# Decoder layer on one core: seven products in four of eight pairs of three input-projection sections, with five low parts made by an adding transfer

## The chip, the cores and the metric

One core of a Trainium2 chip runs the whole program. The metric is the time of one execution in microseconds of device time. The kernel before takes 1112.39 us (median of three runs, 1111.93 to 1112.93).

## The reference

One layer: block-sparse attention (with 256 positions it is one causal block), then a SwiGLU network, each followed by a LayerNorm. What matters here is the first product, `x @ w_qkv` in float32.

```
q, k, v = jnp.split(x @ w_qkv, 3, axis=-1)          # x 256 x 2048, w_qkv 2048 x 6144
o = moba_attention(q * HEAD_DIM ** -0.5, k, v, rel_bias.T)
x = layer_norm(ALPHA * x + o @ w_o, ln1_g, ln1_b)
x = layer_norm(ALPHA * x + (silu(x @ w_gate) * (x @ w_up)) @ w_down, ln2_g, ln2_b)
```

## The kernel before, in words

**Products.** Every float32 operand is split into a high part `hi` (rounded to float32r by ScalarE) and a low part `lo` = value minus `hi` (VectorE). A product is three matmuls of 128x512 into one PSUM bank: hi by hi, lo by hi, hi by lo (lines 317 to 319, or 381 to 385 where plain sections write them out).

**Sections and pairs.** The input projection has six sections Q0 to Q5; each makes two 512-wide column chunks for 256 rows of x. The inner dimension is walked in eight *pairs* p0 to p7 of two 128-deep steps. Sections Q1, Q2 and Q3 (the table `SEVEN`) and the gate sections f1 to f10 of the feed-forward part work on combined operands: an ordinary pair there takes eight products (four in each of two *blocks*), a pair listed in the section's table `st` takes seven (three in its first block, four in its second). Results land in seven accumulators, numbered 1 to 7; at the end of a section `sums_1` (accumulators 1, 6, 7), `sums_2` (2, 4) and `sums_3` (5, 3) add them up on VectorE. Accumulators 1, 6 and 7 are written by the seven-product pairs alone, so `sums_1` is queued behind the last such pair.

**Weights.** An ordinary pair is prepared by `plain`: SyncE loads two raw tiles of 512 KB, `split_piece` splits each: ScalarE writes `wh_...`, VectorE subtracts and writes `wl_...`. A seven-product pair is prepared in three steps, `quad_sums` (four additions of 128x512, lines 280 to 283, into `t13` and `t24`), `quad_raw` (splits into `gq`, `uq`) and `quad_low` (splits into `aq`, `bq`). In gate sections f1 to f10 the second chunk of pairs 0 and 5 (`ADDED`) has its low part made in another way: ScalarE writes `hi`, then minus `hi` into the low tile, and a transfer issued by GpSimd adds the weights from memory onto it.

**Left operands.** `combine_x(p)` makes differences of x for each pair, three small VectorE additions and one split more for a pair in the table (lines 331 to 333). It runs during Q0.

**Order.** All is issued from one list of blocks; each engine executes its instructions in that order and waits on semaphores. A step of preparation is queued a fixed number of blocks ahead of the pair's first block: in Q sections 3 for an ordinary pair, 4, 3 and 2 for the three steps of a seven-product pair; in the gate sections after f1 it is 5, and 6, 5 and 4. Tiles of 128x1024 come from 38 buffers, raw tiles from 6.

Of the kernel before, what the change touches and what calls it, by code (L numbers as in the profile page):

```python
# [40 lines left out]
SQK, SV = {0: 0, 1: 2, 2: 4, 3: 5}, {1: (0, 1), 3: (2, 3)}  # L41
SEVEN = (1, 2, 3)
KEEP = 2
ST_Q = (1, 3, 5)
ST_F = (1, 3, 4, 6)
ADDED = (0, 5)
WARM = 9
LEAD = {("d", 0): 6, ("d", 1): 4}
# [4 lines left out]
def decoder_layer(ctx: ExitStack, tc: tile.TileContext, x, xt, rel_bias, w_qkv, w_o, g1, b1, gb1,  # L53
# [9 lines left out]
    def p4(shape, dt, name):  # L63
        return sb.tile(shape, dt, tag="p4", bufs=P4, name=name)
# [19 lines left out]
    def f32(t):  # L84
        return t.bitcast(F)

    def split(hi, lo, src):
        nc.scalar.activation(hi, src, AF.Copy)  # L88
        nc.vector.tensor_tensor(lo, src, f32(hi), op=OP.subtract)  # L89
# [85 lines left out]
        hi, lo = hS[kt // 4]  # L175
        return hi[:, kt % 4, m * P:(m + 1) * P], lo[:, kt % 4, m * P:(m + 1) * P]

    xC, x1C = {"st": ST_Q}, {"st": ST_F}
    Q = [Sec(f"q{n}", [(w_qkv, 4 * i + g) for i, g in pair], 8, x_lhs, xC if n in SEVEN else None)
         for n, pair in enumerate(QKV)]  # L180
    WO = [Sec(f"o{i}", [(w_o, 2 * i + c) for c in range(2)], 8, o_lhs) for i in range(2)]
# [69 lines left out]
    def load_piece(s, p, c):  # L251
        w, col = s.chunks[c]
        r = sb.tile([P, 2, CW], F, tag="raw", bufs=RAW, name=f"r_{s.name}_{p}_{c}")
        src = w[p, col]
        if s is not Q[0] or p:
            nc.sync.dma_start(r, src)
        s.raws[p, c] = r, src

    def split_piece(s, p, c):
        if (p, c) not in s.raws:  # L260
            load_piece(s, p, c)
        r, src = s.raws.pop((p, c))
        hi = p4([P, 2, CW], R, f"wh_{s.name}_{p}_{c}")
        lo = p4([P, 2, CW], R, f"wl_{s.name}_{p}_{c}")
        if s.st == ST_F and c == 1 and p in ADDED:
            nc.scalar.activation(hi, r, AF.Copy)
            nc.scalar.activation(lo, f32(hi), AF.Copy, scale=-1.0)
            nc.gpsimd.dma_start(lo, src, accum_op=OP.add)
        else:
            split(hi, lo, r)  # L270
        s.pieces[p, c] = (hi, lo)
# [33 lines left out]
    def plain(s, p):  # L305
        if s is Q[0]:
            load_x(p, slice(0, 2))
            split_x(p, slice(0, 2))
        for c in range(len(s.chunks)):
            split_piece(s, p, c)  # L310
# [402 lines left out]
    for g in range(4):  # L713
        s = Q[SQK[g]]
# [74 lines left out]
    s = Q[0]  # L789
# [14 lines left out]
    for t, blk in enumerate(blocks):  # L804
        for f, a in pre.get(t, []):
            f(*a)
        while n < len(order) and order[n][0] <= t:
            _, _, p, what, ss = order[n]
# [54 lines left out]
```

## Time and profile before

| what | value |
|---|---|
| median of three runs | 1112.39 us |
| the profiled execution's own time | 1111.51 us |
| its span in the trace | 1109.7 us |
| TensorE busy | 1090.3 us, 98% |
| VectorE busy | 864.6 us, 78% |
| ScalarE busy | 605.5 us, 55% |
| mean granted TensorE clock | 0.996 of full |

How to read it: the profiled execution ran 0.88 us under the median, and 1.8 us of its time lie outside the span. TensorE is busy nearly all the time, so time is saved where it has fewer matmuls and lost where it stands still.

### The profile page before, as it was taken

The page shows a single profiled execution, that of the slowest core. Times are in us where ns is not written, and L with a number is a line of the kernel's source. Part 1 is how long each engine was busy: PE and PEld are TensorE (multiplying, and loading weights), DVE is VectorE, ACT ScalarE, POOL GpSimd, SP SyncE. Part 2 cuts the span into 40 slices and gives each one's busy share as a digit, 9 for nine tenths or more (in the row PEclk, how much of TensorE's full clock was granted, in tenths as well). Part 3 has the DMA queues.
Part 4 walks back from the last instruction along what each step waited for, and adds up shares of the span by engine and source line. Part 5 has one row for each costly group of instructions (what it writes and reads, how often), then busy time and mean ns, then how long its engine had stood idle before and what let it go on. Part 6 is the DMA issues. An engine that isn't in the chain of part 4 may idle for free.

```text
span 1109.7 us, 13827 instructions
## 1 busy us (share of the span) xinstructions
PE 1090.3 (98%) x4992; PEld 901.2 (81%) x4992; DVE 864.6 (78%) x1154; ACT 605.5 (55%) x781; POOL 27.9 (3%) x36
## 2 busy tenths in 40 slices
PE   9999999999999998999999999999999999999995
PEld 6888888888888886888888888888888888888884
DVE  6899785667778669999899999999899555674446
ACT  6564552555655457757657657657657343353410
POOL 0000000000000000000000000000000000000001
PEclk9999999999999999999999999999999999999998
DMA  9665575465656637868768768768768674578512
GB/s 345 197 235 200 204 242 176 138 196 181 216 190 226 246 107 232 257 228 270 240 195 286 240 208 273 237 207 276 230 233 314 215 316 171 231 281 292 201 38 76
DMA packets 69205, 245.42 MB, mean 221 GB/s; under 512 B 7888, under 2 KB 8336, under 8 KB 69136
## 3 DMA queue, kind: packets, MB, share of 16 engines
q1 hardware_dynamic: 63488, 224.06, 57.1%
q0 software_dynamic: 3488, 12.61, 5.7%
q10 hardware_dynamic: 2160, 7.87, 1.7%
q8 instruction: 39, 0.64, 0.2%
q14 instruction: 30, 0.25, 0.1%
HBM read 234.51 MB, written 9.99 MB: 220 GB/s over the span
## 4 chain that ended last, share of the span: by engine, by line
PE 91%; DVE 3%; ACT 2%; DMA 2%; issue 1%; SPq 0%; POOL 0%; ACTq 0%; POOLq 0%; DVEq 0%
PE acc_f L318 12%; PE acc_f L319 12%; PE acc_f L317 12%; PE acc_d L382 7%; PE acc_d L381 7%; PE acc_d L385 7%; PE acc_q L319 4%; PE acc_q L318 4%; PE acc_q L317 4%; PE acc_q L381 4%; PE acc_q L382 4%; PE acc_q L385 4%; PE acc_o L381 2%; PE acc_o L385 2%; PE acc_o L382 2%; DMA wl_f<-in_w_up 1%
## 5 line engine op out<-in xcount | busy, mean ns | idle before, releaser
L89 DVE TENSOR_TENSOR wl_d<-r_d,wh_d 128x1024 fp32r<-128x1024 f32 x88 | 104.6, 1222 | 71.9 <-ACT wh_d L88 49.5
L381 PE MATMUL acc_d<-wh_d,hh 128*128 128x512 f32 x352 | 137.0, 389 | 0.0
L382 PE MATMUL acc_d<-wl_d,hh 128*128 128x512 f32 x352 | 136.9, 389 | 0.0
L88 ACT ACTIVATE wh_d<-r_d 128x1024 fp32r<-128x1024 f32 x88 | 90.2, 1056 | 74.3 <-DMA r_d<-in_w_down 46.1
L385 PE MATMUL acc_d<-wh_d,hl 128*128 128x512 f32 x352 | 99.9, 389 | 0.0
L89 DVE TENSOR_TENSOR wl_q<-r_q,wh_q 128x1024 fp32r<-128x1024 f32 x76 | 89.6, 1220 | 11.9 <-ACT wh_q L88 11.1
L318 PE MATMUL acc_f<-wl_f,x1h 128*128 128x512 f32 x240 | 93.5, 390 | 3.3 <-DMA wl_f<-in_w_up 3.3
L317 PE MATMUL acc_f<-wh_f,x1h 128*128 128x512 f32 x240 | 95.3, 397 | 0.0
L89 DVE TENSOR_TENSOR wl_f<-r_f,wh_f 128x1024 fp32r<-128x1024 f32 x76 | 89.7, 1218 | 6.4 <-ACT wh_f L88 5.9
L319 PE MATMUL acc_f<-wh_f,x1l 128*128 128x512 f32 x240 | 93.6, 390 | 0.0
L88 ACT ACTIVATE wh_f<-r_f 128x1024 fp32r<-128x1024 f32 x76 | 76.6, 1050 | 6.3 <-ACT hT L675 3.2
L385 PEld LDWEIGHTS acc_d<-wh_d,hl 128*128 128x128 f32 x352 | 66.1, 188 | 13.7
L381 PEld LDWEIGHTS acc_d<-wh_d,hh 128*128 128x128 f32 x352 | 66.1, 188 | 13.7
L88 ACT ACTIVATE wh_q<-r_q 128x1024 fp32r<-128x1024 f32 x76 | 75.9, 1048 | 2.3 <-DMA r_q<-in_w_qkv 2.1
L382 PEld LDWEIGHTS acc_d<-wl_d,hh 128*128 128x128 f32 x352 | 66.1, 188 | 13.7
L381 PE MATMUL acc_q<-wh_q,xh 128*128 128x512 f32 x184 | 73.9, 402 | 0.0
L382 PE MATMUL acc_q<-wl_q,xh 128*128 128x512 f32 x184 | 72.0, 391 | 1.0 <-DVE wl_q L89 1.0
L88 ACT ACTIVATE aq<-t 128x1024 fp32r<-128x1024 f32 x49 | 51.6, 1053 | 35.5 <-DVE t L281 32.0
L89 DVE TENSOR_TENSOR aq<-t,aq 128x1024 fp32r<-128x1024 f32 x49 | 59.6, 1217 | 2.0 <-ACT aq L88 2.0
L89 DVE TENSOR_TENSOR bq<-t,bq 128x1024 fp32r<-128x1024 f32 x49 | 59.6, 1217 | 0.0
L385 PE MATMUL acc_q<-wh_q,xl 128*128 128x512 f32 x184 | 56.9, 390 | 0.0
L318 PEld LDWEIGHTS acc_f<-wl_f,x1h 128*128 128x128 f32 x240 | 45.1, 188 | 12.3 <-DMA wl_f<-in_w_up 3.6
(271 smaller groups left out, 2515.9 us busy)
## 6 DMA issues: line engine op xcount, KB each, us to landing
r_q<-in_w_qkv SPq DMA_DIRECT2D x94, 512.0 KB, 4.3
r_f<-in_w_gate SPq DMA_DIRECT2D x88, 512.0 KB, 5.1
r_f<-in_w_up SPq DMA_DIRECT2D x88, 512.0 KB, 5.9
r_d<-in_w_down SPq DMA_DIRECT2D x88, 512.0 KB, 6.1
r_o<-in_w_o SPq DMA_DIRECT2D x32, 512.0 KB, 4.5
wl_f<-in_w_up POOLq DMA_DIRECT2D x20, 512.0 KB, 9.1
hd<-hT ACTq DMA_DIRECT2D x9, 512.0 KB, 4.3
hT<-hd SPq DMA_DIRECT2D x9, 512.0 KB, 3.5
```

Source lines behind the costliest of these rows:

```text
L88: nc.scalar.activation(hi, src, AF.Copy)
L89: nc.vector.tensor_tensor(lo, src, f32(hi), op=OP.subtract)
L317: nc.tensor.matmul(a, lh, rh, start=start, stop=False)
L318: nc.tensor.matmul(a, lh, rl, start=False, stop=False)
L319: nc.tensor.matmul(a, ll, rh, start=False, stop=stop)
L381: nc.tensor.matmul(a, lh, hi[:, k, :], start=kt == 0, stop=False)
L382: nc.tensor.matmul(a, lh, lo[:, k, :], start=False, stop=False)
L385: nc.tensor.matmul(s.acc[m, c], ll, hi[:, k, :], start=False, stop=kt == nk - 1)
```

## The change

Sections Q1 to Q3 take the table of the gate sections: pairs 1, 3, 4 and 6 take seven products, where it was 1, 3 and 5. In these sections the second chunk of pairs 0 and 5 gets its low part by the adding transfer, except pair 0 of Q1: five transfers, issued by GpSimd. The gate sections are as before. Lines below the tables move up by one.

```diff
-ST_Q = (1, 3, 5)
-ST_F = (1, 3, 4, 6)
+SEVENS = (1, 3, 4, 6)
 ADDED = (0, 5)
...
-    xC, x1C = {"st": ST_Q}, {"st": ST_F}
+    xC, x1C = {"st": SEVENS}, {"st": SEVENS}
...
-        if s.st == ST_F and c == 1 and p in ADDED:
+        if s.st and c == 1 and p in ADDED and (p or s is not Q[1]):
             nc.scalar.activation(hi, r, AF.Copy)
             nc.scalar.activation(lo, f32(hi), AF.Copy, scale=-1.0)
             nc.gpsimd.dma_start(lo, src, accum_op=OP.add)
```

In the rows below a name reads: kind, `q` for an input section, pair, chunk, number of the tile. ScalarE in Q1 stands so from pair 4 on, before:

```order
L88 ACTIVATE wh_q_4_0_646<-r_q_4_0_644 128x1024
L88 ACTIVATE wh_q_4_1_652<-r_q_4_1_650 128x1024
L88 ACTIVATE gq<-r_q_5_0_668 128x1024
L88 ACTIVATE uq<-r_q_5_1_670 128x512
L88 ACTIVATE aq<-t_672 128x1024
L88 ACTIVATE bq<-t_673 128x1024
L88 ACTIVATE wh_q_6_0_729<-r_q_6_0_727 128x1024
```

and of the change:

```order
L87 ACTIVATE gq<-r_q_4_0_638 128x1024
L87 ACTIVATE uq<-r_q_4_1_640 128x512
L87 ACTIVATE aq<-t_642 128x1024
L87 ACTIVATE bq<-t_643 128x1024
L87 ACTIVATE wh_q_5_0_699<-r_q_5_0_697 128x1024
L265 ACTIVATE wh_q_5_1_705<-r_q_5_1_703 128x1024
L266 ACTIVATE wl_q_5_1_706<-wh_q_5_1_705 128x1024
L87 ACTIVATE gq<-r_q_6_0_722 128x1024
```

Pair 5's high parts, and the new negated copy `wl_q_5_1`, now stand behind `bq` of pair 4, whose input is the last of VectorE's four additions for pair 4. The same order stands in Q2 and Q3. VectorE at the end of Q1 and the start of Q2, before (L405 is `sums_1`, L411 `sums_2`, `t_829` belongs to pair 1 of Q2):

```order
L89 TENSOR_TENSOR wl_q_7_1_769<-r_q_7_1_766,wh_q_7_1_768 128x1024
L405 TENSOR_TENSOR v_785<-v_784,acc_q_6_617 128x512
L406 TENSOR_TENSOR v_785<-v_785,acc_q_7_610 128x512
L89 TENSOR_TENSOR wl_q_0_0_804<-r_q_0_0_801,wh_q_0_0_803 128x1024
L89 TENSOR_TENSOR wl_q_0_1_810<-r_q_0_1_807,wh_q_0_1_809 128x1024
L280 TENSOR_TENSOR t_829<-r_q_1_0_825,r_q_1_1_827 128x512
```

and of the change:

```order
L88 TENSOR_TENSOR wl_q_7_0_784<-r_q_7_0_781,wh_q_7_0_783 128x1024
L88 TENSOR_TENSOR wl_q_7_1_790<-r_q_7_1_787,wh_q_7_1_789 128x1024
L88 TENSOR_TENSOR wl_q_0_0_817<-r_q_0_0_814,wh_q_0_0_816 128x1024
L404 TENSOR_TENSOR v_840<-v_839,acc_q_6_623 128x512
L405 TENSOR_TENSOR v_840<-v_840,acc_q_7_616 128x512
L279 TENSOR_TENSOR t_848<-r_q_1_0_844,r_q_1_1_846 128x512
```

`sums_1` moved behind the low part of Q2's pair 0, and the subtraction `wl_q_0_1` is gone; the additions for pair 1 follow `sums_1` directly. GpSimd, before the change, has only the bias loads here; of the change:

```order
L267 DMA wl_q_5_1_706<-in_w_qkv 128x1024
L267 DMA wl_q_0_1_823<-in_w_qkv 128x1024
L267 DMA wl_q_5_1_1057<-in_w_qkv 128x1024
L267 DMA wl_q_0_1_1174<-in_w_qkv 128x1024
L267 DMA wl_q_5_1_1408<-in_w_qkv 128x1024
L147 DMA bias_1545<-rows 128x4x256
```

The five transfers stand ahead of the first bias load: pair 5 of Q1, pairs 0 and 5 of Q2, pairs 0 and 5 of Q3.

## Rows read from the trace of the kernel before

**Rows 1.** The page: busy time of each engine; the last chain by engine.

```profile
PE 1090.3 (98%) x4992; PEld 901.2 (81%) x4992; DVE 864.6 (78%) x1154; ACT 605.5 (55%) x781; POOL 27.9 (3%) x36
...
PE 91%; DVE 3%; ACT 2%; DMA 2%; issue 1%; SPq 0%; POOL 0%; ACTq 0%; POOLq 0%; DVEq 0%
```

**Rows 2.** Windows: stretch, length, busy time per engine, clock, DMA share, GB/s.

```profile
50.00:175.00 125.00, 125.00 (x554) 103.48 (x553) 105.28 (x124) 66.64 (x75) 0.82 (x1) 1.00 0.62 209
443.00:450.00 7.00, 7.00 (x31) 5.79 (x32) 6.93 (x11) 1.70 (x2) 0.00 (x0) 1.00 0.52 198
459.00:467.00 8.00, 8.00 (x37) 6.64 (x36) 7.97 (x10) 6.53 (x8) 0.88 (x1) 1.00 0.96 261
```

**Rows 3.** Timeline of TensorE: first matmuls of Q1, Q1's pair 5, and Q2.

```profile
52.14 0.39 PE L317 MATMUL acc_q<-wh_q,xh 128*128 128x512 f32 x1
...
77.98 0.39 PE L317 MATMUL acc_q<-gq,xh 128*128 128x512 f32 x1
...
93.62 0.39 PE L317 MATMUL acc_q<-wh_q,xh 128*128 128x512 f32 x1
```

**Rows 4.** Timeline of VectorE: two combines, a seven-product pair, two low parts.

```profile
42.43 0.40 DVE L324 TENSOR_TENSOR xd<-xr 128x256 f32<-128x256 f32 x1
...
44.39 0.42 DVE L89 TENSOR_TENSOR xdl<-xd,xdh 128x256 fp32r<-128x256 f32 x1
...
50.11 0.42 DVE L324 TENSOR_TENSOR xd<-xr 128x256 f32<-128x256 f32 x1
51.02 0.42 DVE L89 TENSOR_TENSOR xdl<-xd,xdh 128x256 fp32r<-128x256 f32 x1 [0.48 <-ACT xdh L88]
...
61.19 0.69 DVE L280 TENSOR_TENSOR t<-r_q,r_q 128x512 f32<-128x512 f32 x1
...
63.73 1.22 DVE L89 TENSOR_TENSOR gq<-r_q,gq 128x1024 fp32r<-128x1024 f32 x1
...
67.73 2.35 DVE L89 TENSOR_TENSOR wl_q<-r_q,wh_q 128x1024 fp32r<-128x1024 f32 x2
```

**Rows 5.** Timeline of VectorE at the end of Q1.

```profile
82.33 0.69 DVE L405 TENSOR_TENSOR v<-v,acc_q 128x512 f32<-128x512 f32 x1 [1.16 <-PE acc_q L319]
...
83.66 2.35 DVE L89 TENSOR_TENSOR wl_q<-r_q,wh_q 128x1024 fp32r<-128x1024 f32 x2
...
90.42 0.69 DVE L411 TENSOR_TENSOR v<-v,acc_q 128x512 f32<-128x512 f32 x1 [1.87 <-PE acc_q L319]
...
97.51 1.22 DVE L89 TENSOR_TENSOR wl_q<-r_q,wh_q 128x1024 fp32r<-128x1024 f32 x1
```

**Rows 6.** Timeline of ScalarE: Q1's pair 3, and an adding low part of f1.

```profile
63.90 1.06 ACT L88 ACTIVATE bq<-t 128x1024 fp32r<-128x1024 f32 x1
64.87 2.00 ACT L88 ACTIVATE wh_q<-r_q 128x1024 fp32r<-128x1024 f32 x2
...
430.53 1.04 ACT L266 ACTIVATE wh_f<-r_f 128x1024 fp32r<-128x1024 f32 x1
431.60 1.06 ACT L267 ACTIVATE wl_f<-wh_f 128x1024 fp32r<-128x1024 f32 x1
```

**Rows 7.** The last chain in order of time: start, us, what.

```profile
432.97 9.92 DMA wl_f<-in_w_up
```

**Rows 8.** Tile wl_f: issue to landing of the twenty adding transfers.

```profile
DMA to landing us min/median/max: 7.3/9.1/10.5
```

**Rows 9.** The same, quickest and slowest of pair 5's ten (issued 459.17, 541.62).

```profile
DMA to landing us min/median/max: 7.6/7.6/7.6
...
DMA to landing us min/median/max: 9.8/9.8/9.8
```

**Rows 10.** Line 148: issue to landing of the four bias loads.

```profile
DMA to landing us min/median/max: 5.1/5.5/6.1
```

**Rows 11.** Timeline of TensorE: f1's first adding low part; the warm-up.

```profile
442.94 0.50 PE L318 MATMUL acc_f<-wl_f,x1h 128*128 128x512 f32 x1 [3.31 <-DMA wl_f<-in_w_up]
...
1.19 3.69 PE L117 MATMUL warm<-zero 128*128 128x512 bf16 x9 [1.19 <-DVE zero L114]
```

## The prediction

> **What bounds the kernel now.** The page comes first: TensorE is busy for 98% of the span, and the last chain runs through it for 91% [rows 1]. So the rows to read are those that give its time per matmul, and those where it stands still. The windows show no gap at all over Q1 to Q3: 125.00 us busy in 125.00, at full granted clock, with VectorE at 105.28 us [rows 2]. From the timeline of TensorE, Q1 starts at 52.14 and Q2 at 93.62 [rows 3]; between lie 5 ordinary pairs of eight products and 3 of seven, 61 products or 183 matmuls: 41.48 / 183 = 0.2267 us a matmul, 0.680 us a product. (The 0.39 of a row is the passage of one matmul; they overlap.) The one long stall that an adding transfer causes in this kernel is at f1: TensorE idle 3.31 us [rows 11].
>
> **What is removed.** In each of three sections one pair more takes seven products: 3 products or 9 matmuls less, 9 x 0.2267 = 2.04 us. TensorE being the bound, all of it counts. It is 0.18% of the time, just under the 0.2% (2.2 us) that a measurement here can tell from no change. The change cannot be measurably faster by this term, so all hangs on what it delays.
>
> **VectorE's work.** A seven-product pair occupies it from 61.19 to 67.73, 6.54 us; two low parts of an ordinary pair take 2.27 (the second starts 2.35 - 1.22 = 1.13 after the first) [rows 4]. Per section the trade adds 6.54 - 2.27 = 4.27; each adding transfer takes off 1.13. That is +3.14 in Q1 and +2.01 in Q2 and Q3: 112.4 of some 123 us. In sum it fits; the order decides.
>
> **Pair 5 of Q1.** The added combine work for pair 6 falls just ahead of Q1's first low parts: from its first subtraction to its last split 44.39 - 42.43 = 1.96 us with the three additions, 51.02 - 50.11 = 0.91 without [rows 4], so +1.05 (pair 5's combine loses as much as pair 4's gains, earlier in Q0). VectorE then runs without a gap, and pair 3's additions start at 61.19 + 1.05 = 62.24, pair 4's at 62.24 + 6.54 = 68.78. ScalarE's `bq` starts 63.90 - 61.19 = 2.71 after a pair's first addition, and its next instructions of this size follow 64.87 - 63.90 = 0.97 apart [rows 4, 6]: `bq` of pair 4 at 71.49, the two high parts of pair 5 at 72.46 and 73.43, the negated copy 431.60 - 430.53 = 1.07 later at 74.50 [rows 6], and GpSimd's transfer 432.97 - 431.60 = 1.37 after that [rows 6, 7]: 75.87. TensorE wants it soon: in before its fifth pair starts at 77.98 [rows 3]; now pair 4 starts at 77.98 - 8 x 0.680 = 72.54, pair 5 at 72.54 + 7 x 0.680 = 77.30, its second block, which reads this chunk, four products later at 80.02, and the first matmul with the low part at 80.25. From issue to need: 4.38 us. Call the time from issue to landing L; the stall is L - 4.38.
>
> **Pair 5 of Q2 and Q3.** Let T be the section's start on TensorE. Before, the first low part of Q2's pair 2 starts at 97.51 = T + 3.89 [rows 3, 5]. `sums_1` started at 82.33, which is 0.41 ahead of the end of pair 5 (77.98 + 7 x 0.680 = 82.74) [rows 3, 5]. Now it follows pair 6, with one ordinary pair (5.44 us) still to come: T - 5.85. Behind it on VectorE stand the four additions of pair 1, 63.73 - 61.19 = 2.54 [rows 4], and then everything that ran from 90.42 to 97.51 without a gap, 7.09; `sums_1` itself takes 83.66 - 82.33 = 1.33 [rows 5]. So pair 2's low parts start at T - 5.85 + 1.33 + 2.54 + 7.09 = T + 5.11, pair 4's additions 2.27 + 6.54 later at T + 13.92, `bq` at T + 16.63, and the transfer, by the same 0.97 + 0.97 + 1.07 + 1.37, at T + 21.01. Pair 5 starts after 37 products, 25.16, and wants the low part at 25.16 + 2.72 + 0.23 = T + 28.11. From issue to need: 7.10 us; the stall is L - 7.10, twice.
>
> **Pair 0 of Q2 and Q3** has time. In Q1 pair 6's additions start at 68.78 + 6.54 + 1.13 = 76.45, `bq` at 79.16, then come four high parts (3.88), the copy and the issue: 85.48. Without stalls it is wanted at 93.62 - 0.68 + 2.95 = 95.89, 10.4 us later, and pair 5's stall adds to that. In Q3 the same count gives 13.1 us. Both cost nothing; if this cover were gone, each would cost L less what is left of it.
>
> **Other parts at no cost.** `sums_1` comes later, and Q2's second accumulator takes a bank that it frees, but it ends at T - 4.52 and the bank is written first at T + 0.68. The bias loads behind the transfers on GpSimd are still ahead of their use by a section. Pair 4's `gq` low part in Q1 ends at 68.78 + 2.54 + 1.22 = 72.54 and is wanted at 72.77: 0.23 us of cover, the thinnest; were VectorE later by some d, the transfer would be later by the same d, so d counts once.
>
> **The price of L.** Twenty adding transfers in the gate sections took 7.3 to 10.5 us, median 9.1 [rows 8]; the ten for pair 5 took 7.6 to 9.8 [rows 9], with a mean of 8.5. The nearest kin are these: same size, same place in the section. The share of the DMA engines was 0.96 around one of them and is 0.62 over Q1 to Q3 [rows 2], which speaks for the lower half, while the last chain shows a first one at 9.92 [rows 7]. I take 8.5. Below 4.38 no transfer would stall anything; the quickest transfers that GpSimd issues at all, the bias loads that add nothing, took 5.1 to 6.1 [rows 10].
>
> The Trainium skill (DMA: Bandwidth & Descriptors, section "Anatomy of one DMA — SWDGE (gpsimd) path") gives 2.0 us plus bytes / 436e3 for a transfer on this path; 512 KB would be an estimated 3.2 us, no pair would stall, and the sum would be a plain gain of 2.04. The trace does not agree: 7.3 us is the least it shows for an adding transfer, and 5.1 for a plain one.
>
> **The sum.** (L - 4.38) + 2 (L - 7.10) - 2.04 = 3 L - 20.62. For L = 8.5: 4.12 + 1.40 + 1.40 - 2.04 = +4.88. On the profiled execution's 1111.51 that is 1116.4; the median lies 0.88 above it: **1117.3 us**. For L = 7.3 the sum is +1.3, for 10.5 it is +10.9.
>
> **The rivals.**
> *Quick landing: not slower.* If in these quieter sections L is under 7.61, the sum is under 2.2 us and nothing can be measured; it decides at L = 6.87, where it is zero. For it speaks the DMA share of 0.62, against it that only one of twenty, in the emptied last section, was under 7.6. About 1113.5.
> *Hidden transfers.* Every landing under 4.38, as by the rule above: 1112.39 - 2.04 = 1110.3. Against it stand all rows on GpSimd's transfers.
> *VectorE becomes the bound.* If waits for ScalarE or for freed buffers delay its run of 33 us in a section by 1 us each, the sum is 3 us higher: 1120.3. For it: only 0.23 us of cover in Q1. Against: it ran there without a gap before.
> *The clock falls in the stall.* At L = 8.5 TensorE is idle in Q1 for some 4 us. After the 3.31 us at f1 the granted clock was 1.00, the 2.4 GHz level, over the next 7 us [rows 2, 11]. Longer idling is not shown. The warm-up matmuls took 3.69 / 9 = 0.41 us each [rows 11] against 0.227; nine such matmuls would cost 1.7 us more: 1119.0. The Trainium skill (TensorE: Matmul & The Clock Gate, Part 1) says that an idle stretch can bring the clock down to 1.2 GHz; the 3.31 us here did not.
>
> **How the numbers follow.** The forecast, L from 7.61 to 10.5: 0.66. Quick landing 0.14, hidden 0.07 (in 0.03 of it some other gain makes it measurable), VectorE 0.08, the clock 0.05. Slower by over 0.2%: 0.66 + 0.08 + 0.05 = 0.79; within: 0.14 + 0.04 = 0.18; faster 0.03. The forecast's own range is 1114.6 (L = 7.61) to 1123.3 (L = 10.5). For 8 in 10 I leave out the hidden case, the quickest landings and the slowest tail: 1112.5 to 1122.0.
>
> **What would show it.** TensorE waits for `wl_q` from a transfer three times, some 4 us in Q1 and 1 to 2 us in Q2 and Q3, always at pair 5's second block; none at pair 0. GpSimd issues at about 75.9 and at T + 21.0. Pair 2's low parts in Q2 start at T + 5.1. Wrong would be: landings under 7 us; waits for VectorE in place of transfers; stalls at other pairs.

## The result and the profile after

The changed kernel takes 1119.13 us (median of six runs, 1116.58 to 1121.68), the kernel before, in runs beside it, 1112.33 (1111.26 to 1112.93). The ratio is 1.0064, 95% interval [1.0051, 1.0076]: slower by 6.80 us.

The profiled execution of the changed kernel took 1121.68 us, with a span of 1119.9; it is the longest of the six. The page first, busy time and last chain, to be read beside [rows 1]:

```profile
PE 1093.8 (98%) x4983; PEld 902.2 (81%) x4983; DVE 872.4 (78%) x1171; ACT 615.9 (55%) x793; POOL 32.2 (3%) x41
...
PE 79%; DVE 8%; DMA 5%; issue 5%; ACT 3%; SPq 0%; POOL 0%; ACTq 0%; DVEq 0%; POOLq 0%
```

The nine matmuls are gone (4992 to 4983), and yet TensorE is busy for longer, 1093.8 in place of 1090.3 us: some matmuls ran slowly. Transfers now have 5% of the last chain, where it was 2%. The windows, in the columns of [rows 2]: Q1 to Q3, the 8.8 us after Q1's transfer, the matmuls right behind Q1's stall, the start of f1, and the matmuls right behind its stall.

```profile
50.00:175.00 125.00, 118.11 (x513) 96.67 (x512) 110.02 (x136) 75.22 (x86) 5.12 (x6) 0.99 0.68 217
75.90:84.70 8.80, 4.57 (x21) 3.44 (x19) 8.77 (x11) 6.06 (x7) 0.85 (x1) 0.97 0.93 289
84.73:88.00 3.27, 3.27 (x9) 2.61 (x9) 1.75 (x2) 2.11 (x2) 0.61 (x1) 0.56 1.05 370
...
440.00:480.00 40.00, 36.37 (x153) 29.60 (x152) 34.10 (x41) 27.77 (x32) 2.24 (x3) 0.91 0.78 249
450.44:456.45 6.01, 6.01 (x14) 4.71 (x15) 5.87 (x9) 1.69 (x2) 0.00 (x0) 0.51 0.45 181
```

Where TensorE had no gap, 6.89 of 125 us are idle now, and the granted clock is 0.99 there and 0.91 at f1; right behind the two stalls it is 0.56 and 0.51. What TensorE waited for (sum, times, longest):

```profile
PE acc_q L317 <- DMA wl_q<-in_w_qkv: 6.9, 3, 4.3
PE acc_f L317 <- DMA wl_f<-in_w_up: 3.6, 1, 3.6
```

The first row is new. The second is the stall that [rows 11] show with 3.31 us. The timeline of TensorE at pair 5 of Q1, Q2 and Q3, and at f1:

```profile
80.08 0.39 PE L316 MATMUL acc_q<-wh_q,xh 128*128 128x512 f32 x1
84.73 0.79 PE L317 MATMUL acc_q<-wl_q,xh 128*128 128x512 f32 x1 [4.26 <-DMA wl_q<-in_w_qkv]
85.32 0.63 PE L318 MATMUL acc_q<-wh_q,xl 128*128 128x512 f32 x1
...
88.00 0.40 PE L316 MATMUL acc_q<-wh_q,xdh 128*128 128x512 f32 x1
...
128.29 0.50 PE L317 MATMUL acc_q<-wl_q,xh 128*128 128x512 f32 x1 [1.10 <-DMA wl_q<-in_w_qkv]
...
170.90 0.50 PE L317 MATMUL acc_q<-wl_q,xh 128*128 128x512 f32 x1 [1.52 <-DMA wl_q<-in_w_qkv]
...
450.44 0.80 PE L317 MATMUL acc_f<-wl_f,x1h 128*128 128x512 f32 x1 [3.63 <-DMA wl_f<-in_w_up]
451.04 0.63 PE L318 MATMUL acc_f<-wh_f,x1l 128*128 128x512 f32 x1
...
456.45 0.40 PE L316 MATMUL acc_f<-gq,x1h 128*128 128x512 f32 x1
```

A matmul that passes in 0.63 us instead of 0.39 follows its forerunner by 0.43 instead of 0.227: with the granted clock of 0.56 and 0.51 that is the 1.2 GHz level. After Q1's stall eight matmuls take from 84.73 to 88.00, 3.27 us where 8 x 0.2267 = 1.81 would do: 1.46 lost. At f1 fourteen take 6.01 us for 3.17: 2.84 lost, behind a stall that in the profile of before had no such sequel (clock 1.00, [rows 2]).

So the profiled execution stands against the forecast for it, 1116.4: the 1.46 and the 2.84, and f1's stall longer by 0.32, make 1121.0, which is 0.7 short of 1121.68. The rest lies in how the rows count. The idle time of a row begins where the matmul ahead ends its 0.39 us, but the next one was due 0.227 us after that one's start. So each delay is 0.16 longer than its row: 4.42, 1.26 and 1.68 us, 7.36 together. And the first matmuls behind a stall lose some 0.15 us at full clock too (before, fourteen from 442.94 on took 3.32 us), so that about 1.3 of the 1.46 and 2.7 of the 2.84 are the clock's. Whole stretches agree. The last block of Q3, after and then before:

```profile
182.39 0.39 PE L316 MATMUL acc_q<-wh_q,xh 128*128 128x512 f32 x1
...
175.22 0.39 PE L317 MATMUL acc_q<-wh_q,xh 128*128 128x512 f32 x1
```

Counted from Q1's first matmul (52.16, and 52.14 before) it comes 7.15 us later, with the nine matmuls already taken off; f1's 0.32 and 2.7 on top make 10.2 us, the whole difference between the spans.

### The profile page after: what moved, and what is told of

It is laid out like the page before. It is cut to its first block, busy times and chain, and to the rows that moved or that the text cites. A ratio compares the mean times of both kernels' runs of the same rounds, so it can differ in the third digit from the quotient of the medians.

```text
span 1119.9 us, 13861 instructions
## 1 busy us (share of the span) xinstructions
PE 1093.8 (98%) x4983; PEld 902.2 (81%) x4983; DVE 872.4 (78%) x1171; ACT 615.9 (55%) x793; POOL 32.2 (3%) x41
## 4 chain that ended last, share of the span: by engine, by line
PE 79%; DVE 8%; DMA 5%; issue 5%; ACT 3%; SPq 0%; POOL 0%; ACTq 0%; DVEq 0%; POOLq 0%
PE acc_f L317 12%; PE acc_f L318 12%; PE acc_f L316 12%; PE acc_d L381 7%; PE acc_d L380 7%; PE acc_d L384 7%; PE acc_q L380 3%; PE acc_q L381 3%; PE acc_q L384 3%; DMA wl_q<-in_w_qkv 2%; PE acc_o L380 2%; PE acc_o L384 2%; PE acc_o L381 2%; DVE wl_q L88 1%; DMA r_q<-in_w_qkv 1%
## 5 line engine op out<-in xcount | busy, mean ns | idle before, releaser
L88 DVE TENSOR_TENSOR wl_q<-r_q,wh_q 128x1024 fp32r<-128x1024 f32 x65 | 76.9, 1222 | 12.0 <-ACT wh_q L87 11.4
L87 ACT ACTIVATE aq<-t 128x1024 fp32r<-128x1024 f32 x52 | 54.8, 1054 | 37.7 <-DVE t L280 37.2
L87 ACT ACTIVATE wh_q<-r_q 128x1024 fp32r<-128x1024 f32 x65 | 65.3, 1048 | 4.0 <-DMA r_q<-in_w_qkv 4.0
L88 DVE TENSOR_TENSOR aq<-t,aq 128x1024 fp32r<-128x1024 f32 x52 | 63.4, 1219 | 4.9 <-ACT aq L87 4.9
L88 DVE TENSOR_TENSOR bq<-t,bq 128x1024 fp32r<-128x1024 f32 x52 | 63.4, 1219 | 0.0
L87 ACT ACTIVATE bq<-t 128x1024 fp32r<-128x1024 f32 x52 | 54.8, 1053 | 5.3 <-DVE t L282 4.6
```

## The experiments

All kernels come from the changed one, if nothing else is said. Two theories stood against each other at first. **A**: the loss is TensorE waiting for pair 5's transfers, and the low clock that such waits can leave behind. **B**: the loss is VectorE's added work. A third, **C**, says that the low clock at f1 belongs to the old stall there and not to the change.

**e1: no adding transfer in Q1 to Q3.**

```diff
-        if s.st and c == 1 and p in ADDED and (p or s is not Q[1]):
+        if s in FU[1:] and c == 1 and p in ADDED:
```

> Four seven-product pairs as in the change, but no adding transfer in Q1 to Q3: VectorE makes all low parts there. Theory A (the loss is TensorE waiting for pair 5's transfers, and the low clock after it): nothing is left but the 9 fewer matmuls, 1112.3 - 2.0 = 1110.3, within 1109.5 to 1112, and no wait for a transfer before f1. Theory B (the loss is VectorE's added work for the fourth seven-product pair and the later sums): VectorE has 1.13 us more per transfer taken out, so the kernel is at least as slow as the changed one, 1119 or more, with TensorE waiting for VectorE in Q1 to Q3.

Measured: 1109.80 us (1107.70 to 1111.00) against 1112.53 of the kernel before in the same set, 0.9974 [0.9964, 0.9985]. VectorE has more to do than in the changed kernel (877.9 us against 872.4), and TensorE's longest waits are these:

```profile
PE acc_f L317 <- DMA wl_f<-in_w_up: 3.1, 1, 3.1
PE warm L116 <- DVE zero L113: 1.2, 1, 1.2
```

None of them is in Q1 to Q3. B falls: four seven-product pairs with all their VectorE work are 2.7 us faster than before, where A wanted 2.0.

**e4: without the transfer of Q1's pair 5.**

```diff
-        if s.st and c == 1 and p in ADDED and (p or s is not Q[1]):
+        if s.st and c == 1 and p in ADDED and s is not Q[1]:
```

> The change without the one transfer of Q1's pair 5; Q2 and Q3 keep theirs. Theory A: Q1's stall of 4.26 us and the slow stretch of 1.46 us behind it go, the two stalls of 1.1 and 1.5 stay: 1112.3 - 2.0 + 2.6 = 1112.9 with f1 as in the kernel before, up to 1116 if the clock falls at f1 too. Theory B: 1119, as the changed kernel. Rival C (the slow stretch at f1 belongs to the longer wait there alone and not to the change): f1's 2.8 us come and go whatever Q1 does, so single times lie up to 2.8 apart.

Measured: 1113.44 (1109.98 to 1116.49), ratio 1.0014 [1.0002, 1.0025], by A's number. The two stalls left:

```profile
PE acc_q L317 <- DMA wl_q<-in_w_qkv: 2.0, 2, 1.5
```

It is 0.91 us above the kernel before where the changed kernel is 6.80: one transfer of five, Q1's pair 5, is 5.9 us of it. The single times lie 6.5 apart, more than C's 2.8; two more stalls at which the clock can fall are in it.

**e5: pair 5's second chunk queued two blocks earlier.**

```diff
                 todo = [(f - (3 if s in Q else 4 if s is FU[1] and not p else 5), "plain")]
+                if s in Q and p == 5:
+                    todo = [(f - 5, "added"), *todo]
...
+            if (p, c) not in s.pieces:
                 split_piece(s, p, c)
+
+    def added(s, p):
+        split_piece(s, p, 1)
```

> All five transfers stay, but in Q1 to Q3 the second chunk of pair 5 (high part, negated copy, transfer) is queued two blocks earlier, ahead of aq and bq of pair 4, so that it no longer waits behind VectorE's additions. Theory A: GpSimd issues Q1's at about 69.9 in place of 75.85; with 8.9 us to landing that is 78.8, before the need at 80.3, and Q2's and Q3's have some 5 us more as well. No stall: 1110.3, to 1113 if the clock falls at f1. Theory B: 1119, since VectorE's work is the same. If a transfer issued earlier takes longer (the queue is what is full), the stalls stay.

Measured: 1110.60 (1108.13 to 1111.28), ratio 0.9979 [0.9970, 0.9988]. ScalarE does the high part and the negated copy in a gap between `uq` and `aq` of pair 4, where it had idled, and GpSimd issues at 69.76. Its timeline, and the time to landing of all five:

```profile
69.76 0.90 POOL L269 DMA_DIRECT2D wl_q<-in_w_qkv  x1 [25.27 <-ACT wl_q L268]
85.34 0.86 POOL L269 DMA_DIRECT2D wl_q<-in_w_qkv  x1 [14.68 <-DVE wl_q L88]
107.80 0.85 POOL L269 DMA_DIRECT2D wl_q<-in_w_qkv  x1 [21.59 <-ACT wl_q L268]
...
DMA to landing us min/median/max: 6.3/7.3/9.8
```

TensorE waits for none of them; only f1's stall (3.15 us) is left. All five transfers are there, and the loss is gone: it was the place in ScalarE's order. (The edit moves the chunk's SyncE load as well; GpSimd's issue, in both kernels, is released by ScalarE's `wl_q`.) What costs is a landing behind the need, not the transfers as such.

**e6: pair 5's transfers do not add.**

```diff
+            if p == 5 and s in Q:
+                nc.gpsimd.dma_start(lo, src)
+            else:
                 nc.gpsimd.dma_start(lo, src, accum_op=OP.add)
```

> Pair 5's three transfers in Q1 to Q3 stay where they are but do not add: the low part of that chunk is the weights themselves, which leaves the subtraction of the high part out of the result. It measures what the adding costs in time to landing. Theory A with the adding as the price: they land in about 5.5 us as the bias loads do, Q1's stall is 5.5 - 4.4 = 1.1, none in Q2 and Q3, 1111.5. If the price is the transfer's size or GpSimd's queue and not the adding: 8.9 us to landing, 1119 as the changed kernel. If landing comes under 4.4 us: no stall, 1110.3. Theory B: 1119.

Measured: 1114.08 (1110.14 to 1116.68), ratio 1.0010 [0.9998, 1.0022], between the two numbers of A. The time to landing was neither of the two that were expected, 5.5 and 8.9 us: the three plain transfers landed after 7.4, 6.8 and 7.4 us, the two adding ones of pair 0 in the same kernel after 9.6 each. The rows of Q1's plain one, of an adding one, and the stalls:

```profile
75.50 0.59 POOL L268 DMA_DIRECT2D wl_q<-in_w_qkv  x1 [31.30 <-ACT wl_q L266]
...
DMA to landing us min/median/max: 7.4/7.4/7.4
...
DMA to landing us min/median/max: 9.6/9.6/9.6
...
PE acc_q L320 <- DMA wl_q<-in_w_qkv: 2.9, 1, 2.9
PE acc_f L320 <- DMA wl_f<-in_w_up: 2.1, 1, 2.1
```

By the prediction's term Q1's stall is 7.4 - 4.38 = 3.02; the row has 2.86, which with the 0.16 is a delay of 3.0. So the term holds at a second value of L. The adding is the smaller part of L: at these three places the changed kernel, e4, e7 and e8 made eleven adding transfers that landed after 7.2 to 9.6 us, 8.5 on average, against 7.2 for the plain ones. Some of the eleven were no slower than those, so 1.3 us is a mean and not a fixed price. Most of L a plain transfer of GpSimd's takes too, while SyncE's loads of the same 512 KB land after a median of 4.6 us in this run. The Trainium skill (DMA: Bandwidth & Descriptors, "Anatomy of one DMA — SWDGE (gpsimd) path") would have an estimated 3.2 us for a plain transfer of this size; 6.8 to 7.4 were measured.

**e7: TensorE kept busy in the two long waits.**

```diff
         if s.comb is not None:
+            n = {("q1", 5, 1): 15, ("f1", 0, 1): 12}.get((s.name, pairs[0], m), 0)
+            if n:
+                b = bank("keep")
+                for _ in range(n):
+                    nc.tensor.matmul(b, zero[:, :P], zero, start=True, stop=True)
+                give(b)
             half_block(s, pairs[0], m)
```

> The change as it is, but TensorE fills most of its two long waits with matmuls that nobody reads: 15 (3.4 us) ahead of the second block of Q1's pair 5, 12 (2.7 us) ahead of the second block of f1's pair 0. The transfers land no sooner, so the real work waits as long as before. Theory A (the low clock behind a long wait is some 2 us of the loss, on top of the waits): the matmuls behind both waits run at full clock, the sum without a clock term 1112.5 - 2.0 + 6.9 = 1117.4 or a little under, and the single times lie within about 2 us. If the clock has no part in it: 1119 and single times 5 apart, as the changed kernel.

Measured: 1115.81 (1115.69, 1115.80, 1115.81, 1116.23 and, the profiled one, 1118.46) against 1112.35, ratio 1.0036 [1.0023, 1.0048]. The kernel is 3.3 us faster than the changed one. The timeline of TensorE in Q1, and at pair 5 of Q2:

```profile
80.29 3.41 PE L371 MATMUL keep<-zero 128*128 128x512 bf16 x15
83.35 0.58 PE L316 MATMUL acc_q<-wh_q,xh 128*128 128x512 f32 x1
85.65 0.50 PE L317 MATMUL acc_q<-wl_q,xh 128*128 128x512 f32 x1 [1.72 <-DMA wl_q<-in_w_qkv]
85.98 0.39 PE L318 MATMUL acc_q<-wh_q,xl 128*128 128x512 f32 x1
...
128.80 0.50 PE L317 MATMUL acc_q<-wl_q,xh 128*128 128x512 f32 x1 [2.06 <-DMA wl_q<-in_w_qkv]
129.14 0.39 PE L318 MATMUL acc_q<-wh_q,xl 128*128 128x512 f32 x1
...
130.06 0.63 PE L318 MATMUL acc_q<-wh_q,xdl 128*128 128x512 f32 x1
```

In Q1 the real matmuls pass in 0.39 us behind the wait, and so they do at f1. In this one execution the clock fell behind Q2's wait, which was not filled: from 129.37 nine matmuls take 3.65 us for 2.04, 1.6 of some 2.5 us by which this execution is longer than the other four.

The waits were not the same as in the changed kernel's profile: Q1's transfer landed after 9.6 us (8.8 there), f1's after 8.3 (10.2 there), so that the real work came 0.7 us later in Q1 and 1.2 earlier at f1, where the filling covered the whole wait. That the low clock is a cost of its own, on top of the waits, is shown by the rows: the same matmuls follow each other by 0.43 us behind the unfilled wait and by 0.23 behind Q1's, filled but for 1.72 us. How much of the 3.3 us it is, this run does not separate. The kernel came out 1.6 us under the expected 1117.4. That sum started from the 1112.5 of before, which holds on average 1.3 us of low clock at f1 (e11); the filling takes that away too.

**e8: VectorE makes the low part of f1's pair 0.**

```diff
-        if s.st and c == 1 and p in ADDED and (p or s is not Q[1]):
+        if s.st and c == 1 and p in ADDED and (p or s not in (Q[1], FU[1])):
```

> The change, with one transfer less: VectorE makes the low part of f1's pair 0, second chunk, in 1.13 us. The stall of some 3 us there is in the kernel before as well. Rival C (the low clock at f1 hangs on that stall alone): the stall and the 2.8 us of slow matmuls behind it go, 1119.1 - 3.3 - (up to 2.8) = 1113 to 1116, and the single times lie closer. If VectorE, which has no gap there, hands the stall on: within 1.1 us of 1119.

Measured: 1115.12 (1113.52 to 1116.38) against 1112.35, ratio 1.0023 [1.0014, 1.0032]: 4.0 us less than the changed kernel. f1's stall and its slow matmuls are gone, VectorE hands nothing on, and the single times lie 2.9 apart instead of 5.1. What is left is in Q1 and Q3 (Q2's transfer landed after 7.2 us, and nothing waited):

```profile
PE acc_q L317 <- DMA wl_q<-in_w_qkv: 5.3, 2, 4.0
```

**e11: the same edit in the kernel before.**

```diff
-        if s.st == ST_F and c == 1 and p in ADDED:
+        if s.st == ST_F and c == 1 and p in ADDED and (p or s is not FU[1]):
```

> The kernel before with one edit: VectorE in place of the adding transfer at f1's pair 0. It says what that old stall and the low clock behind it cost without the change. If they cost the stall and, on average, half of the slow stretch: 1112.4 - 3.3 - 1.0 = 1108.1, single times within 1.5 us of each other, in place of 4 and more. Taken with the runs that have the same edit and four seven-product pairs without stalls (1105.9 and 1106.6), theory A wants it 2.0 us above them: 1107.9 to 1108.6. If VectorE hands the stall on: 1111.

Measured: 1107.98 (1107.69 to 1108.31) against 1112.76, ratio 0.9961 [0.9947, 0.9975]. The old stall costs 4.8 us in the kernel before: 3.5 of delay (the row's 3.31 and the 0.16) and on average 1.3 more. The single times of before reach from 1110.26 to 1114.89 over the 54 runs beside e1 to e13, those of this kernel over 0.6 us. The mean granted clock of each run says the same: it was 0.996 in 15 of the 54, and these are the 15 quickest (up to 1111.71); in the other 39, from 1111.97 up, it was 0.993 to 0.995. All 54 average 1.3 us above those 15. C holds: f1's low clock comes and goes without the change, and the profiled execution of before (1111.51, clock 0.996) is like the minority that it spared.

**e10, e13 and e9: four seven-product pairs without late transfers.** All have VectorE at f1's pair 0. e10 has no adding transfer in Q1 to Q3, e13 only those of pair 0 in Q2 and Q3, e9 all five, with the order of e5.

```diff
-        if s.st and c == 1 and p in ADDED and (p or s is not Q[1]):
+        if s in FU[1:] and c == 1 and p in ADDED and (p or s is not FU[1]):                                                     # e10
+        if s.st and c == 1 and p in ADDED and (p == 0 and s in Q[2:] or p == 5 and s in FU or p == 0 and s in FU[2:]):          # e13
+        if s.st and c == 1 and p in ADDED and (p or s not in (Q[1], FU[1])):                                                    # e9, with e5's edit
```

> No adding transfer in Q1 to Q3 (that alone gave 1109.8), and none for f1's pair 0: VectorE makes these low parts. 1109.8 - 3.1 = 1106.7 if the stall goes, 1108.7 or more if VectorE hands it on.

> Pair 0's two transfers in Q2 and Q3 alone: those of pair 5 in Q1 to Q3 and f1's pair 0 go back to VectorE. If pair 0 has the time that the prediction counted (10 and 13 us from issue to need): no wait, and 1106.5 as without any transfer there (1106.55), within 0.5. If pair 0's transfers delay other loads on the DMA engines and these TensorE: 1108 or more.

> Pair 5's transfers queued two blocks earlier (the run of that edit alone gave 1110.6 against 1112.5), and VectorE in place of the transfer at f1's pair 0. If the two stalls are separate: 1110.6 - 3.1 = 1107.5, with no wait over 1 us left and no slow stretch. If VectorE hands f1's stall on: 1109 to 1110.

Measured: e10 1106.55 (1106.27 to 1106.86), 0.9948 [0.9935, 0.9962]; e13 1106.13 (1105.90 to 1106.55), 0.9944 [0.9932, 0.9957]; e9 1105.87 (1105.44 to 1106.54), 0.9942 [0.9929, 0.9954]. e9 beats both kernels, by 6.5 and 13.3 us. e9 is 1.6 us under its expected 1107.5, which had counted f1's stall as 3.1 where e11 has 4.8. Set against e11 they gain 1.4, 1.9 and 2.1 us, but only e13 ran beside it; each taken against the kernel before of its own runs, the gains are 1.0, 1.9 and 1.7. Only e10 differs from e11 in the seventh products alone (e13 and e9 have transfers for VectorE's work as well). With intervals of about 1.4 us to either side they agree with the 2.04 of the prediction and do not fix it. e9's waits of TensorE, the first three, and below them the wait at pair 0 in e13:

```profile
PE warm L116 <- DVE zero L113: 1.2, 1, 1.2
PE acc_q L387 <- DVE wl_q L88: 0.9, 2, 0.6
PE t L451 <- DVE k L403: 0.8, 1, 0.8
```

```profile
PE acc_q L317 <- DMA wl_q<-in_w_qkv: 0.2, 1, 0.2
...
DMA to landing us min/median/max: 9.6/9.6/9.7
```

## Why the prediction was right, and where it was off

The forecast was 1117.3 and slower; 1119.13 lies 1.8 above it and in the range. Its steps one by one, against the changed kernel's trace.

**What is removed** holds: the account of the profiled execution above closes with it, and e10, e13 and e9 against e11 agree within their noise (1.0 to 2.1).

**Pair 5 of Q1** holds to a few hundredths. Timelines of VectorE (Q1 and the start of Q2), TensorE (Q2's first matmul) and ScalarE, and GpSimd's issues:

```profile
62.23 0.69 DVE L279 TENSOR_TENSOR t<-r_q,r_q 128x512 f32<-128x512 f32 x1
...
68.77 0.69 DVE L279 TENSOR_TENSOR t<-r_q,r_q 128x512 f32<-128x512 f32 x1
...
93.07 0.69 DVE L404 TENSOR_TENSOR v<-v,acc_q 128x512 f32<-128x512 f32 x1 [6.58 <-PE acc_q L318]
...
103.92 1.22 DVE L88 TENSOR_TENSOR wl_q<-r_q,wh_q 128x1024 fp32r<-128x1024 f32 x1
...
98.92 0.39 PE L316 MATMUL acc_q<-wh_q,xh 128*128 128x512 f32 x1
```

```profile
71.48 1.06 ACT L87 ACTIVATE bq<-t 128x1024 fp32r<-128x1024 f32 x1 [0.27 <-DVE t L282]
72.45 1.04 ACT L87 ACTIVATE wh_q<-r_q 128x1024 fp32r<-128x1024 f32 x1
73.40 1.04 ACT L265 ACTIVATE wh_q<-r_q 128x1024 fp32r<-128x1024 f32 x1
74.47 1.06 ACT L266 ACTIVATE wl_q<-wh_q 128x1024 fp32r<-128x1024 f32 x1
```

```profile
75.85 0.90 POOL L267 DMA_DIRECT2D wl_q<-in_w_qkv  x1 [31.31 <-ACT wl_q L266]
...
119.79 0.85 POOL L267 DMA_DIRECT2D wl_q<-in_w_qkv  x1 [31.54 <-ACT wl_q L266]
...
161.99 0.86 POOL L267 DMA_DIRECT2D wl_q<-in_w_qkv  x1 [30.15 <-ACT wl_q L266]
...
DMA to landing us min/median/max: 8.5/8.9/9.7
```

The additions of pairs 3 and 4 start at 62.23 and 68.77 (62.24 and 68.78 were worked out), `bq` waits for the last of them and starts at 71.48 (71.49), the transfer goes out at 75.85 (75.87). Reading the order of one engine together with another's durations gave the stall's place and start to 0.02 us.

**Pair 5 of Q2 and Q3** holds as well. `sums_1` starts at 93.07 after waiting 6.58 us for the accumulators; Q2 starts at 98.92 on TensorE, so pair 2's low part at 103.92 is T + 5.00 (T + 5.11 was worked out) and the issue T + 20.87 (21.01).

**The price of L** was taken as 8.5; pair 5's three landed after 8.8, 8.5 and 8.9. With the eight of e4, e7 and e8 at the same places the mean is 8.5, as taken. The stalls, 4.12 + 1.40 + 1.40 = 6.92 by the formula, were 4.26 + 1.10 + 1.52 = 6.88 in the rows and 7.36 as delays. That one execution came so near is in part luck, since the transfers at these places took from 7.2 to 9.6 us. And one argument for the choice was wrong: the share of the DMA engines of 0.62 over Q1 to Q3 is a mean, and in the 8.8 us after Q1's issue the share was 0.93. Nor does the share order the landings: in e5 the three of pair 5 took 7.3, 6.3 and 6.9 us while the share was 0.95, 1.01 and 1.00. What makes one transfer take 5.5 (e9, pair 5 of Q3) and another 9.8 stays open. A smaller slip: the bias loads are the quickest of GpSimd's transfers of 512 KB, not of all; the 24 KB of `rows` landed after 2.4 us.

**Pair 0** waited for nothing, in the changed kernel and in e5, where no stall delays TensorE: Q2's was issued there at 85.34 (85.48 was worked out) and landed 9.8 us later, within the 10.4 of the count. The cover is thin, though: in e13, where VectorE makes pair 5's low part as well, 1.13 us more, the issue was at 86.7 and TensorE waited 0.2 us.

**VectorE becomes the bound** fell with e1.

**The clock** is where the size was off. The forecast left it out, on the ground that "the 3.31 us here did not" bring it down. That was one execution, and like the 15 in 54 that the fall spared; e11 puts its average cost there at 1.3 us. In Q1 the fall cost 1.3 of the 1.46 in the profiled run (the rival had 1.7), and e7, which keeps TensorE busy, takes 3.3 us off the two places together, landings included. The forecast with the 1.46 is 1118.8, and the median is 1119.1. In how many executions the clock fell in Q1 no trace counts, but e8, which has no stall at f1, points to most: its mean clock was 0.993 to 0.995 in its eleven runs, where e9 and e10, without stalls, have 0.996 and 0.997 in their ten. (One run of e11 has 0.995 without a stall, so the clock of a single run is a hint and no proof.) So the rival described what happened, and its 1119.0 lies nearer the median than the forecast's 1117.3; that it lies within 0.1 is luck, with single times from 1116.58 to 1121.68. Its chance of 0.05 was far too small.

## What to carry to other kernels

A low part that comes by a transfer must be issued its whole time to landing ahead of its use, and in order engines decide when that is: here the transfer stood behind an activation that waited for another engine, and queuing the chunk's two activations and its transfer ahead of that one turned a loss of 6.8 us into a gain of 2. Price a stall of TensorE above its length where it is some microseconds long, since the matmuls behind it may run slowly, and look for such stalls that are there already: the one at f1 was worth 4.8 us, over twice what the nine matmuls save. A clock that held in one profiled execution is no evidence that it holds in the next.

## What the runs showed of the hardware

The length of an idle stretch did not order which ones were followed by the 1.2 GHz level. In the profiled runs the clock fell after an idle time of 2.06 us (e7, Q2), 2.13 (e6, f1), 3.15 (e5, f1), 3.63 and 4.26 (the changed kernel) and 3.98 (e8, Q1), and it did not fall after 2.86 (e6, Q1), 2.88 (e4, f1), 3.05 (e1, f1) and the 3.31 of before. Two windows of f1's start, one of each kind (length, TensorE busy, clock, DMA share, GB/s), e1 and e5:

```profile
440.00:480.00 40.00, 38.76 (x173) 1.00 0.86 282
```

```profile
440.00:480.00 40.00, 39.26 (x168) 0.96 0.83 271
```

The Trainium skill (TensorE: Matmul & The Clock Gate, Part 1) says that an idle stretch can bring the clock down, and the runs agree with that much; by its length alone they could not be told apart.

Adding transfers of 512 KB landed after 7.2 to 9.6 us at pair 5's three places (eleven, in the changed kernel, e4, e7 and e8), 1.3 us later on average than the three plain ones of e6. Issued earlier in the section, six of them landed after 5.5 to 7.5 us (e5 and e9). A plain one landed over 2 us later than SyncE's loads of that size (e6: 6.8 to 7.4 against a median of 4.6).
